# Gate granules shared by the two chunks of a pair, the second chunk one tile behind

## The chip, the cores and the metric

The kernel runs on one core of a Trainium2 chip. The metric is device time of one execution in microseconds (us). Before the change three executions took 1790.26, 1792.09 and 1793.38 us; their median is 1792.09 us.

## What is computed

Two residual layers over a sequence of 2048 rows of width 1024, in float32. Each layer is a token mixer (layer 0: a gated short convolution, layer 1: a gated causal pooling), followed by a gated embedding:

```python
for i in range(DEPTH):                       # DEPTH = 2
    hn = rmsnorm(h, norm_mix[i])
    h = h + (short_conv_mixer if i == 0 else pool_mixer)(hn, ...)
    gate = jax.nn.sigmoid(rmsnorm(h, ple_norm[i]) @ ple_w_gate[i])
    h = h + gate * (p[i] @ ple_w_proj[i])
return rmsnorm(h, final_norm)
```

The change concerns the product with `ple_w_gate[i]`, a 1024 x 1024 matrix, called the gate below.

## The kernel before

Everything is held transposed: features on the 128 partitions, rows of the sequence along the free dimension. The sequence is cut into 4 chunks of 512 columns; the two halves of the outer loop (`sc`) take two chunks each, so there are four pairs: layer 0 and layer 1 of each half. A float32 product is made of three float32r matmuls: both operands are split into a high and a low part (`mm`, L276 to L278, uses high x high, high x low, low x high).

Weights come in granules of 128 x 1024 (512 KB). A list, `order`, written out by hand, says in which order. `next_granule` takes the next one and loads ahead by `look[0]` granules: an SP DMA into one of 4 raw buffers, a cast on ACT for the high part (L117), a subtraction on DVE for the low part (L118). The split granules live in a ring of 4 buffers (`wring`), 8 KB per partition each.

Stages of one pair: the mixer's products, a filler (the products p @ w_proj of another chunk, evacuated by ACT, L763, and stored to DRAM), `mixer_out` (the mixer's output product for both chunks at once, adds into h on DVE, L727; it also makes the scaled split operands a[0], a[1] of the gate with L310 on ACT and L311 on DVE), the gates, another filler. `gate` runs one chunk: for each of 8 granules `dense_w` makes 24 matmuls of 128 x 128 by 128 x 512 into one PSUM bank, and `gate_out` evacuates it: multiply by the norm on DVE (L780), sigmoid on ACT (L781), times the embedding (fetched from DRAM, L782), add into h (L783). After that `Stat.add` accumulates squares (ACT L331, POOL L334), and a callback makes the operand for the next stage: in layer 0 a scaled split of h (L310, L311), in layer 1 of the first half `X.ahead`, which fetches one of 28 operands of the next half's mixer from DRAM (n<-ndr) and splits it (ACT L304, DVE L305). The second chunk's gate loads the same 8 granules again.

The root of a norm is made in two steps, `fin1` (ACT cast acc_hi L339, DVE L341, two matmuls `tot` L344, then L350 to L360 on DVE with L355 on POOL) and `fin2` (matmul `bc` L365, ACT copy `rb` L367). Both matmuls write the one bank of the PSUM pool `pst`. They are put into a list, `hooks`, and each `dense_w` runs the first one left in it. `mixer_out` leaves [fin2 of the first chunk, fin1 of the second, nop, fin2 of the second]. In layer 1 `finals` adds to fin2 eight scalings on DVE (L813), each with a store to the output.

The pools: 7 PSUM banks for products, 31 tiles of 4 KB per partition (`acts`) shared by h (4 tiles for a chunk), the split operands (one tile for each of 8 k's and chunk) and the next stage's operands; 4 buffers `nx` for tiles fetched from DRAM. The order within each engine's queue is drawn up by the tile framework at build time with a timeline simulation, from the order in which the program emits instructions; on the chip each engine but PE's weight load runs its queue in that order.

Of the kernel before, what the change touches and what calls it, by code (L numbers as in the profile page):

```python
# [18 lines left out]
T = 512  # L19
KT = D // P  # L20
NCH = S // T
# [28 lines left out]
def trunk_kernel(ctx: ExitStack, tc: tile.TileContext, xT, xN, pT, wts, par, out):  # L50
# [189 lines left out]
    for sc in range(2):  # L240
        order += filler_order(0, 2) if sc else []
        order += sum_order(sc, 4)
        for i in range(4, 2 * KT, 2):
            order += fold_order(i // 2 - FOLDS) if sc == 0 and FOLDS <= i // 2 < FOLDS + 4 else []
            order += [("sum", (sc, i + r, part)) for r in range(2) for part in range(4)]
        order += filler_order(0, 3) if sc else filler_order(1, 0)
        order += out_order(0)
        order += [("w", W_GATE[0] + i) for t in range(2) for i in range(KT)]
        order += filler_order(1, 1 + sc)
        order += [g for j in B_ORDER for g in (("comb", j), ("w", W_BZ + j))]  # L250
        order += out_order(1)
        order += [("w", W_GATE[1] + i) for t in range(2 - sc) for i in range(KT)]
    order += [("p", 2 * NCH - 1)]
    for h in range(2):
        order += [("pt", W_GATE[1] + 8 + h)] + [("w", W_GATE[1] + 4 * h + i) for i in range(4)]
# [52 lines left out]
    def split_scaled(h, gcol):  # L308
        a = new_act()
        nc.scalar.activation(out=a[:, 0, :], in_=h, func=AF.Copy, scale=pcol(gcol))  # L310
        nc.vector.scalar_tensor_tensor(out=a[:, 1, :], in0=h, scalar=pcol(gcol), in1=a[:, 0, :].bitcast(F32),  # L311
                                       op0=ALU.mult, op1=ALU.subtract)
        return a
# [237 lines left out]
    class Operands:  # L551
# [5 lines left out]
        def ahead(self, n):  # L557
            for name in self.have:
                while n and len(self.have[name]) < 4:
                    self.have[name].append(self.make(name, len(self.have[name])))  # L560
                    n -= 1
# [204 lines left out]
    def filler(layer, ch, *between):  # L766

        keys = filler_order(layer, ch)
        pt = next_granule(keys[0])
        for h in range(2):  # L770
            ple_half(layer, ch, pt, next_granule(keys[1 + h]), h)
            for f in between[h:h + 1]:
                f()
# [24 lines left out]
    def gate(layer, ch, a, hs, s_in, extra):  # L798
        s = Stat()
        held = []  # L800
        for k in range(KT):
            held.append((k, dense(("w", W_GATE[layer] + k), a), embedded(layer, ch, k)))
            if s_in.rb is None:
                continue
            for kk, g_ps, e in held:
                gate_out(g_ps, e, hs[kk], s_in.rb, 0, T)
                s.add(hs[kk])
                extra(kk)
            held = []
        return s  # L810

    def scale_out(ch, hs, rb, k, c0, c1):
        nc.vector.scalar_tensor_tensor(out=hs[k][:, c0:c1], in0=hs[k][:, c0:c1], scalar=pcol(G_FIN + k), in1=rb,  # L813
                                       op0=ALU.mult, op1=ALU.mult)
        nc.sync.dma_start(out=out[ch, :, k, c0:c1], in_=hs[k][:, c0:c1])

    def finals(ch, hs, s):
        def last():
            s.fin2()
            for k in range(KT):  # L820
                scale_out(ch, hs, s.rb, k, 0, T)
        return [s.fin1, nop, last]

    def gate_last(layer, ch, a, hs, s_in):
        pt = next_granule(("p", layer * NCH + ch))
        base = W_GATE[layer]
        half = T // 2
        ss = [Stat(half), Stat(half)]
        held, ws, wps, roots = [], {}, {}, []
        whole = KT // 2  # L830
        seq = [(k, None) for k in range(whole)]
        for i in range(whole, KT + LAG):
            if i < KT:
                seq.append((i, 0))
            if i >= whole + LAG:
                seq.append((i - LAG, 1))

        on_pool = (1, 3)

        def root(hf):  # L840
            c0, c1 = hf * half, (hf + 1) * half
            for k in on_pool:
                nc.scalar.activation(out=hs[k][:, c0:c1], in_=hs[k][:, c0:c1], func=AF.Copy, scale=pcol(G_FIN + k))
            bc = ss[hf].fin_fast(hs[KT - 1][:, c0:c1])
            rb = rbp.tile([P, T], F32, tag="rb", name="rb")
            nc.scalar.copy(out=rb[:, :half], in_=bc)
            return bc, rb

        def finish(hf, bc, rb, after=None):
            c0, c1 = hf * half, (hf + 1) * half  # L850
            for q in range(2):
                if after:
                    with tc.issue_after(after[q].ins):
                        scaled(hf, c0, c1, bc, rb, q)
                else:
                    scaled(hf, c0, c1, bc, rb, q)

        def scaled(hf, c0, c1, bc, rb, q):
            o = acts.tile([P, 4, half], F32, tag="act", name="o")
            for i in range(4):  # L860
                k = 4 * q + i
                if k in on_pool:
                    nc.gpsimd.tensor_tensor(out=o[:, i, :], in0=hs[k][:, c0:c1], in1=rb[:, :half], op=ALU.mult)
                else:
                    nc.vector.scalar_tensor_tensor(out=o[:, i, :], in0=hs[k][:, c0:c1], scalar=pcol(G_FIN + k),
                                                   in1=bc, op0=ALU.mult, op1=ALU.mult)
            if q == 0:
                nc.sync.dma_start(out=out[ch, :, 0:4, c0:c1], in_=o)
            else:
                for i in range(0, 4, 2):  # L870
                    nc.sync.dma_start(out=out[ch, :, 4 + i:6 + i, c0:c1], in_=o[:, i:i + 2, :])

        def span(hf):
            return (0, T) if hf is None else (hf * half, (hf + 1) * half)

        for k, hf in seq:
            if not hf:
                if k % 4 == 0:
                    wps[k // 4] = next_granule(("pt", base + 8 + k // 4))
                ws[k] = next_granule(("w", base + k))  # L880
            held.append((k, hf) + gate_mm(ws[k], wps[k // 4], pt, a, k, *span(hf)))
            if s_in.rb is None:
                continue
            for kk, h2, g_ps, p_ps in held:
                done = gate_out(g_ps, p_ps, hs[kk], s_in.rb, *span(h2))
                for q in (0, 1) if h2 is None else (h2,):
                    b0, b1 = span(q)
                    if kk == KT - 1:
                        roots.append(root(q))
                    else:  # L890
                        ss[q].add(hs[kk][:, b0:b1], nc.vector)
            held = []
        finish(0, roots[0][1][:, :half], roots[0][1], (done, ss[1].diagonal))
        finish(1, *roots[1])
# [61 lines left out]
    def keep(ch, hs, k):  # L956
        nc.sync.dma_start(out=h_dram[ch][:, k, :], in_=hs[k])

    for sc in range(2):
        chs = (2 * sc, 2 * sc + 1)  # L960
        Y = Outputs(2 * sc, (0, 1, 2, 3))
        mixer_a(sc, X, Y, xT[chs[1]])
        filler(*((0, 3) if sc else (1, 0)))
        a, hs, s = mixer_out(0, Y, xT[chs[0]])
        ab, ss = ([], []), []
        for t, ch in enumerate(chs):
            def after_gate(k):
                ab[t].append(split_scaled(hs[t][k], G_MIX + 8 + k))
                keep(ch, hs[t], k)

            ss.append(gate(0, ch, a[t], hs[t], s[t], after_gate))
            if t == 0:
                hooks.extend([ss[0].fin1, nop, ss[0].fin2])
        filler(1, 1 + sc, ss[1].fin1, ss[1].fin2)

        Y = Outputs(2 * sc + 1, (3, 2, 1, 0))
        mixer_b(ab, ss, Y, sc, nop if sc else between_b, h_dram[chs[1]])
        a, hs, s = mixer_out(1, Y, h_dram[chs[0]])
        if sc == 0:
            X = Operands(second_operand)  # L980

        def ahead(k):
            if sc == 0 and (t == 0 or k % 2):
                X.ahead(1)

        for t, ch in enumerate(chs):
            if ch == NCH - 1:
                look[0] = 1
                gate_last(1, ch, a[t], hs[t], s[t])
                break  # L990
            g = gate(1, ch, a[t], hs[t], s[t], ahead)
            if t == 0:
                hooks.extend(finals(ch, hs[t], g))
                continue
            fin1, _, fin2 = finals(ch, hs[t], g)
            filler(0, 2, fin1, fin2)


# [53 lines left out]
```

## Time and profile before

| | |
|---|---|
| median of 3 executions | 1792.09 us |
| the profiled execution | 1793.33 us |
| its span, first to last instruction | 1791.6 us |
| mean granted clock of PE | 0.995 |
| PE busy | 1757.7 us, 98% |
| DVE busy | 1360.8 us, 76% |
| ACT busy | 757.6 us, 42% |
| DMA traffic | 329.71 MB, mean 184 GB/s |

Busy times are added up over instructions of one engine; PE's matmuls overlap each other. PEld is the weight load of PE. "Idle" of an instruction is the time its engine stood still just before it, and the arrow names what ended that.

### The profile page before, as it was taken

The numbers are of one execution on the slowest core, as the hardware profiler recorded it, in microseconds if no ns is written. First come the engines' busy times: TensorE is split into PE (matmuls) and PEld (weight loads), VectorE is DVE, ScalarE is ACT, GpSimd is POOL, SyncE is SP. The second block draws the span as 40 slices with busy tenths as digits, with TensorE's granted clock in tenths as the row PEclk, the third lists the DMA queues.
The fourth block names the chain that finished last, engine by engine and source line by source line (L and its number), as shares of the span: only waits on it lengthen the run. The fifth ranks groups of instructions, "written<-read, shape, count | busy, mean of one in ns | idle before, by whom it ended". The sixth has DMA issues, their size and how long they took to land.

```text
span 1791.6 us, 21940 instructions
## 1 busy us (share of the span) xinstructions
PE 1757.7 (98%) x7883; PEld 1451.8 (81%) x7883; DVE 1360.8 (76%) x1876; ACT 757.6 (42%) x1142; POOL 230.0 (13%) x216
## 2 busy tenths in 40 slices
PE   9899999999999999999999999999999999999997
PEld 6688888888888888887878888888888888888787
DVE  6897787987987778889786555557798776578876
ACT  6734443355554311455553333334555511135542
POOL 1000000002322000023210000000132200002320
PEclk9999999999999999999999999999999999999998
DMA  9456566795465556844584434348536522365322
GB/s 347 170 185 220 205 233 222 279 361 170 141 200 177 187 190 224 296 146 139 198 270 142 137 104 141 102 160 296 199 125 199 189 95 97 109 223 171 129 90 95
DMA packets 123934, 329.71 MB, mean 184 GB/s; under 512 B 13744, under 2 KB 15792, under 8 KB 123824
## 3 DMA queue, kind: packets, MB, share of 16 engines
q1 hardware_dynamic: 123824, 328.30, 53.1%
q8 instruction: 62, 1.02, 0.2%
q14 instruction: 48, 0.39, 0.1%
HBM read 230.73 MB, written 97.52 MB: 183 GB/s over the span
## 4 chain that ended last, share of the span: by engine, by line
PE 77%; DVE 12%; DMA 5%; issue 3%; ACT 2%; POOL 0%; SPq 0%; DVEq 0%; ACTq 0%; POOLq 0%
PE mm L276 26%; PE mm L277 25%; PE mm L278 25%; DVE w L118 3%; DVE act L311 2%; DVE act L305 2%; DMA n<-ndr 1%; DVE h L727 1%; DMA sdo<-n 1%; ACT w L117 1%; DMA pdr<-wk 1%; DMA n<-in_wts_dram 1%; DMA raw<-in_wts_dram 0%; DVE dg L360 0%; DVE h L579 0%
## 5 line engine op out<-in xcount | busy, mean ns | idle before, releaser
L277 PE MATMUL mm<-act,w 128*128 128x512 f32 (+1 forms) x2400 | 930.7, 388 | 6.0 <-DVE act L305 3.6
L276 PE MATMUL mm<-act,w 128*128 128x512 f32 (+1 forms) x2400 | 923.8, 388 | 4.8 <-ACT wk L436 2.7
L278 PE MATMUL mm<-act,w 128*128 128x512 f32 (+1 forms) x2400 | 920.3, 387 | 0.0
L276 PEld LDWEIGHTS mm<-act,w 128*128 128x128 f32 x2400 | 452.0, 188 | 100.0 <-ACT wk L436 5.1
L277 PEld LDWEIGHTS mm<-act,w 128*128 128x128 f32 x2400 | 451.6, 188 | 100.3 <-DVE act L305 4.9
L278 PEld LDWEIGHTS mm<-act,w 128*128 128x128 f32 x2400 | 451.7, 188 | 91.8 <-issue 0.7
L117 ACT CAST w<-raw 128x1024 fp32r<-128x1024 f32 (+1 forms) x291 | 290.3, 1002 | 499.8 <-PE mm L278 341.0
L118 DVE TENSOR_TENSOR w<-raw,w 128x1024 fp32r<-128x1024 f32 (+1 forms) x291 | 347.2, 1197 | 102.3 <-ACT w L117 98.5
L334 POOL TENSOR_TENSOR acc<-acc,wk 128x512 f32<-128x512 f32 x97 | 139.0, 1433 | 473.4 <-ACT wk L331 473.4
L311 DVE SCALAR_TENSOR_TENSOR act<-h,par_sb,act 128x512 fp32r<-128x512 f32 x108 | 109.9, 1021 | 28.4 <-ACT act L310 26.2
L441 DVE TENSOR_TENSOR wk<-mm,wk 128x512 f32<-128x512 f32 x96 | 66.0, 689 | 85.0 <-PE mm L278 78.8
L331 ACT ACTIVATE wk<-h 128x512 f32<-128x512 f32 (+1 forms) x117 | 70.1, 602 | 102.2 <-DVE h L783 102.2
L310 ACT ACTIVATE act<-h,par_sb 128x512 fp32r<-128x512 f32 x108 | 77.0, 718 | 76.2 <-DVE h L727 72.8
L727 DVE TENSOR_TENSOR h<-mm,h 128x512 f32<-128x512 f32 x112 | 76.1, 685 | 26.1 <-PE mm L278 25.9
L305 DVE TENSOR_TENSOR act<-n,act 128x512 fp32r<-128x512 f32 x112 | 78.1, 724 | 19.2 <-ACT act L304 19.1
L304 ACT CAST act<-n 128x512 fp32r<-128x512 f32 x112 | 65.9, 620 | 61.5 <-DMA n<-ydr 37.5
L436 ACT COPY wk<-mm 128x512 f32<-128x512 f32 x96 | 54.9, 587 | 84.5 <-PE mm L278 81.6
L512 DVE SCALAR_TENSOR_TENSOR wk<-wk,par_sb 128x512 f32<-128x512 f32 x64 | 44.4, 748 | 34.3 <-ACT wk L510 34.3
L697 DVE TENSOR_TENSOR wk<-wk 128x526 f32<-128x526 f32 (+5 forms) x80 | 55.5, 694 | 2.3
L712 ACT ACTIVATE wk<-wk 128x512 f32<-128x512 f32 x32 | 20.2, 631 | 77.3 <-DVE wk L710 77.2
L781 ACT ACTIVATE wk<-wk 128x512 f32<-128x512 f32 (+1 forms) x68 | 40.8, 602 | 25.4 <-DVE wk L780 25.4
L710 DVE TENSOR_TENSOR wk<-mm,rb 128x512 f32<-128x512 f32 x32 | 22.0, 688 | 38.3 <-PE mm L278 38.3
(126 smaller groups left out, 1291.4 us busy)
## 6 DMA issues: line engine op xcount, KB each, us to landing
raw<-in_wts_dram SPq DMA_DIRECT2D x156, 512.0 KB, 3.8
n<-ydr SPq DMA_DIRECT2D x84, 256.0 KB, 4.3
ydr<-y SPq DMA_DIRECT2D x32, 512.0 KB, 3.5
raw<-in_wts_dram SPq DMA_DIRECT2D x64, 256.0 KB, 3.2
raw<-sdo SPq DMA_DIRECT2D x32, 512.0 KB, 6.0
raw<-sda SPq DMA_DIRECT2D x32, 512.0 KB, 3.8
pdr<-wk SPq DMA_DIRECT2D x56, 256.0 KB, 6.1
n<-pdr SPq DMA_DIRECT2D x56, 256.0 KB, 3.6
```

The source lines that it names most:

```text
L117: nc.scalar.copy(out=hi[:, c], in_=raw[:, c])
L118: eng.tensor_tensor(out=lo[:, c], in0=raw[:, c], in1=hi[:, c].bitcast(F32), op=ALU.subtract)
L276: nc.tensor.matmul(out=ps, lhsT=wh, rhs=ah, start=first, stop=False, skip_group_check=skip)
L277: nc.tensor.matmul(out=ps, lhsT=wh, rhs=al, start=False, stop=False, skip_group_check=skip)
L278: nc.tensor.matmul(out=ps, lhsT=wl, rhs=ah, start=False, stop=last, skip_group_check=skip)
L305: nc.vector.tensor_tensor(out=a[:, 1, :], in0=y, in1=a[:, 0, :].bitcast(F32), op=ALU.subtract)
L310: nc.scalar.activation(out=a[:, 0, :], in_=h, func=AF.Copy, scale=pcol(gcol))
L311: nc.vector.scalar_tensor_tensor(out=a[:, 1, :], in0=h, scalar=pcol(gcol), in1=a[:, 0, :].bitcast(F32), op0=ALU.mult, op1=ALU.subtract)
L331: nc.scalar.activation(out=sq, in_=h, func=AF.Square)
L334: (eng or nc.gpsimd).tensor_tensor(out=acc, in0=acc, in1=sq, op=ALU.add)
L441: nc.vector.tensor_tensor(out=o[:, 2:2 + T], in0=ps, in1=c, op=ALU.add)
L727: nc.vector.tensor_tensor(out=hs[t][k], in0=ps, in1=hs[t][k], op=ALU.add)
```

## The change

For three pairs (both layers of the first half, layer 0 of the second) one function, `gate_pair`, replaces the two calls of `gate`. Its products run in the order (granule 0, chunk 0), (1, 0), (0, 1), (2, 0), (1, 1), ... (7, 0), (6, 1), (7, 1). Each granule is loaded once. The look-ahead is 2 granules for the first six and 3 for the last two. The first chunk's norm is put into `hooks` after product (7, 0) without a nop between its steps, so that its fin1 follows (6, 1) and its fin2 (in layer 1 with the eight scalings) follows (7, 1). The fourth pair stays as it was.

```diff
-        order += [("w", W_GATE[0] + i) for t in range(2) for i in range(KT)]
+        order += [("w", W_GATE[0] + i) for i in range(KT)]
...
-        order += [("w", W_GATE[1] + i) for t in range(2 - sc) for i in range(KT)]
+        order += [("w", W_GATE[1] + i) for i in range(KT)]
...
+    def gate_pair(layer, sc, a, hs, s_in, extra, done):
+
+        ss, held, ws = [None, None], ([], []), {}
+        for k, t in [(0, 0)] + [(k - t, t) for k in range(1, KT) for t in range(2)] + [(KT - 1, 1)]:
+            if t == 0:
+                look[0] = 2 if k < KT - 2 else LOOK
+                ws[k] = next_granule(("w", W_GATE[layer] + k))
+            held[t].append((k, dense_w(ws[k], a[t]), embedded(layer, 2 * sc + t, k)))
+            if s_in[t].rb is None:
+                continue
+            for kk, g_ps, e in held[t]:
+                gate_out(g_ps, e, hs[t][kk], s_in[t].rb, 0, T)
+                if kk == 0:
+                    ss[t] = Stat()
+                ss[t].add(hs[t][kk])
+                extra(t, kk)
+            held[t].clear()
+            if (k, t) == (KT - 1, 0):
+                done(ss[0])
+        return ss
...
-        for t, ch in enumerate(chs):
-            def after_gate(k):
-                ab[t].append(split_scaled(hs[t][k], G_MIX + 8 + k))
-                keep(ch, hs[t], k)
-
-            ss.append(gate(0, ch, a[t], hs[t], s[t], after_gate))
-            if t == 0:
-                hooks.extend([ss[0].fin1, nop, ss[0].fin2])
+        ab = [], []
+
+        def after_gate(t, k):
+            ab[t].append(split_scaled(hs[t][k], G_MIX + 8 + k))
+            keep(chs[t], hs[t], k)
+
+        ss = gate_pair(0, sc, a, hs, s, after_gate, lambda g: hooks.extend([g.fin1, g.fin2]))
...
+        if sc == 0:
+            def ends(t, g):
+                fin1, _, fin2 = finals(chs[t], hs[t], g)
+                return fin1, fin2
+
+            def ahead(t, k):
+                if t == 0 or k % 2:
+                    X.ahead(1)
+
+            g = gate_pair(1, sc, a, hs, s, ahead, lambda g: hooks.extend(ends(0, g)))
+            filler(0, 2, *ends(1, g[1]))
+        else:
+            g = gate(1, chs[0], a[0], hs[0], s[0], nop)
+            hooks.extend(finals(chs[0], hs[0], g))
+            look[0] = 1
+            gate_last(1, chs[1], a[1], hs[1], s[1])
```

## Rows read from the trace of the kernel before

**Rows 1.** The page: engines' busy time (share) xinstructions, and chain shares by engine.

```profile
PE 1757.7 (98%) x7883; PEld 1451.8 (81%) x7883; DVE 1360.8 (76%) x1876; ACT 757.6 (42%) x1142; POOL 230.0 (13%) x216
PE 77%; DVE 12%; DMA 5%; issue 3%; ACT 2%; POOL 0%; SPq 0%; DVEq 0%; ACTq 0%; POOLq 0%
```

**Rows 2.** Windows: stretch, length, busy PE, PEld, DVE, ACT, POOL, clock, DMA share, GB/s.

```profile
462.00:558.00 96.00, 95.00 (x419) 78.28 (x418) 84.78 (x106) 51.42 (x77) 28.00 (x19) 1.00 0.52 169
816.00:909.00 93.00, 90.60 (x399) 74.28 (x398) 78.68 (x104) 46.73 (x70) 25.76 (x17) 1.00 0.57 187
909.00:936.00 27.00, 23.93 (x97) 18.96 (x96) 23.10 (x31) 20.35 (x36) 6.24 (x5) 0.94 0.84 267
1317.00:1413.00 96.00, 95.03 (x419) 78.33 (x418) 84.82 (x107) 51.95 (x77) 28.37 (x19) 1.00 0.52 172
```

**Rows 3.** Timeline of PE, starts of pairs 1, 2, 3: start, us, line, [idle before].

```profile
468.55 0.40 PE L365 MATMUL bc<-dg,ones_r 128*128 128x512 f32 x1
474.24 0.39 PE L276 MATMUL mm<-act,w 128*128 128x512 f32 x1
474.47 0.39 PE L277 MATMUL mm<-act,w 128*128 128x512 f32 x1
475.86 0.51 PE L344 MATMUL tot<-acc_hi,ones_r 128*128 128x512 f32 x1 [1.00 <-ACT rb L367]
...
830.20 0.50 PE L344 MATMUL tot<-acc_hi,ones_r 128*128 128x512 f32 x1 [1.00 <-ACT rb L367]
846.87 0.47 PE L365 MATMUL bc<-dg,ones_r 128*128 128x512 f32 x1 [1.40 <-DVE dg L360]
...
1331.98 0.50 PE L344 MATMUL tot<-acc_hi,ones_r 128*128 128x512 f32 x1 [0.97 <-ACT rb L367]
```

**Rows 4.** Timeline of ACT at the start of pair 1.

```profile
473.75 0.62 ACT L339 CAST acc_hi<-acc 128x512 fp32r<-128x512 f32 x1 [2.03 <-DVE acc L334]
474.28 1.04 ACT L117 CAST w<-raw 128x1024 fp32r<-128x1024 f32 x1
475.23 0.58 ACT L367 COPY rb<-bc 128x512 f32<-128x512 f32 x1
```

**Rows 5.** Timeline of DVE, starts of pairs 1 and 2.

```profile
472.38 0.74 DVE L311 SCALAR_TENSOR_TENSOR act<-h,par_sb,act 128x512 fp32r<-128x512 f32 x1
474.41 0.69 DVE L341 TENSOR_TENSOR acc_lo<-acc,acc_hi 128x512 fp32r<-128x512 f32 x1 [0.69 <-ACT acc_hi L339]
...
833.68 0.69 DVE L305 TENSOR_TENSOR act<-n,act 128x512 fp32r<-128x512 f32 x1 [2.08 <-ACT act L304]
837.35 1.23 DVE L118 TENSOR_TENSOR w<-raw,w 128x1024 fp32r<-128x1024 f32 x1 [0.44 <-ACT w L117]
841.61 1.21 DVE L118 TENSOR_TENSOR w<-raw,w 128x1024 fp32r<-128x1024 f32 x1
846.04 0.68 DVE L360 TENSOR_TENSOR dg<-fold,rs 128x512 fp32r<-128x512 f32 x1
```

**Rows 6.** Timeline of PE after pair 2's gates.

```profile
920.02 0.50 PE L276 MATMUL mm<-w 128*128 128x512 f32 x1 [1.16 <-ACT wk L763]
932.27 0.56 PE L276 MATMUL mm<-act,w 128*128 128x512 f32 x1 [1.91 <-ACT wk L763]
933.06 0.63 PE L278 MATMUL mm<-act,w 128*128 128x512 f32 x1
933.49 0.63 PE L276 MATMUL mm<-act,w 128*128 128x512 f32 x1
```

**Rows 7.** Timeline of ACT and DVE around the end of pair 2.

```profile
928.77 1.93 ACT L304 CAST act<-n 128x512 fp32r<-128x512 f32 x3 [3.37 <-DMA n<-ndr]
931.65 2.03 ACT L763 COPY wk<-mm 128x512 f32<-128x512 f32 x4
893.42 6.43 DVE L813 SCALAR_TENSOR_TENSOR h<-h,par_sb,rb 128x512 f32<-128x512 f32 x8
939.58 0.69 DVE L360 TENSOR_TENSOR dg<-fold,rs 128x512 fp32r<-128x512 f32 x1
```

**Rows 8.** Windows of line L305 alone, the splits of the next half's operands.

```profile
816.00:909.00 93.00, 7.53 (x12) 1.00 0.57 187
909.00:945.00 36.00, 12.94 (x16) 0.95 0.78 255
```

More of the change, by code (lines that the diff above doesn't have):

```diff
@@ L964, in trunk_kernel @@
         a, hs, s = mixer_out(0, Y, xT[chs[0]])
-        ab, ss = ([], []), []
-        for t, ch in enumerate(chs):
-            def after_gate(k):
-                ab[t].append(split_scaled(hs[t][k], G_MIX + 8 + k))
-                keep(ch, hs[t], k)
-            ss.append(gate(0, ch, a[t], hs[t], s[t], after_gate))
-            if t == 0:
-                hooks.extend([ss[0].fin1, nop, ss[0].fin2])
+        ab = [], []
[3 more added lines that the diff above has]
+        ss = gate_pair(0, sc, a, hs, s, after_gate, lambda g: hooks.extend([g.fin1, g.fin2]))
         filler(1, 1 + sc, ss[1].fin1, ss[1].fin2)
@@ L980, in trunk_kernel @@
             X = Operands(second_operand)
[L982 to L996, printed above, removed]
+        if sc == 0:
[12 more added lines that the diff above has]
+            gate_last(1, chs[1], a[1], hs[1], s[1])
 def kernel(x, p, norm_mix, a_w_in, a_w_conv, a_w_out, b_w_in, b_w_grp, b_scale, b_w_out,
```

## The prediction

> **What bounds the kernel now.** I read the page's busy shares first. PE is busy 98% of the span, DVE 76%, ACT 42%; the chain that ended last runs 77% through PE [rows 1]. So the change can win or lose only where PE stands still, and the next view is a table of windows over the three stretches that it touches. In the two layer 0 pairs PE is busy 95.00 and 95.03 of 96 us; in pair 2 (layer 1, first half) 90.60 of 93, and in the 27 us behind its gates 23.93, at a granted clock of 0.94 [rows 2]. DMA is at 0.52 to 0.57 in the gates. The whole of PE's idle time there is 1.0 + 2.4 + 1.0 + 3.1 = 7.5 us, and that is the size of the game: 0.4% of 1792 us.
>
> The timeline of PE tells where it lies. Matmuls start 0.227 us apart (474.24 and 474.47), so one product of 24 takes 5.44 us. Each pair has a wait of 1.00, 1.00 and 0.97 us before `tot`, the first matmul of the second chunk's root, released by the copy rb on ACT; pair 2 has another of 1.40 us before `bc`, released by DVE's L360 [rows 3]. The idle column counts from a modelled end 0.39 us after the last start; the next matmul could have started 0.23 us after it, so each wait loses 0.16 us more: 1.16, 1.16, 1.13 and 1.56 us, together 5.0. Behind pair 2's gates PE waits 1.16 and 1.91 us for L763, the filler's evacuation on ACT [rows 6], which is 1.32 + 2.07 us in the same count. After the second wait matmuls start 0.43 us apart (933.06, 933.49: the 1.2 GHz level); my count there is 9 of them, 9 x (0.43 - 0.23) = 1.8 us. So 5.2 us are lost at that place.
>
> **What the change removes.** 24 granules of 512 KB with their casts (L117, 1.04 us of ACT [rows 4]) and subtractions (L118, 1.2 us of DVE [rows 5]): 8 in each pair, 8.3 us of ACT and 9.7 us of DVE out of stretches in which ACT is busy about half and DVE 79 to 85% [rows 2]. PE's 48 products in the three pairs are the same, so no term comes of this by itself: beside PE that work is hidden. It counts only where it stands ahead of something PE waits for.
>
> *Start of each pair.* ACT runs acc_hi 473.75, then a granule's cast at 474.28, then rb at 475.23 [rows 4]; `tot` needs acc_hi and, since the pool `pst` has one bank, the end of rb. The cast between them is the fifth granule's: the ring of 4 buffers lets it in when product (0, 0) has read the first. In the new order the first granule is read until (0, 1) ends, 5.4 us later, so this cast can't stand there. Then rb starts 0.95 us earlier (475.23 - 474.28), and `tot` at about 474.9. I take 0.95 us for each of three pairs, 2.85 us. Ends: 0 (another instruction takes its place ahead of rb) and 1.16.
>
> *The wait of pair 2 before bc.* `tot` runs at 830.20, L360 at 846.04; in between DVE does two such subtractions, 1.23 + 1.21 us, and stands 2.08 us for a fetched operand [rows 5]. The subtractions go (later granules come one in 10.9 us instead of 5.44). That is more than the 1.56 us lost, but the build-time order will also put bc earlier in PE's queue, and the 2.08 us stay. I take half, 0.8 us; ends 0 and 1.56.
>
> **What it adds.** *The second chunk's operands are needed earlier*: product (0, 1) comes third, not ninth. The last tile of a[1] is finished by L311 at 472.38 + 0.74 = 473.1 [rows 5]; (0, 1) starts at about 475 and uses that tile in its last three matmuls, 21 x 0.227 = 4.8 us later. Slack 6.5 us; I cost it at nothing. Were the cover gone, everything beyond 6.5 us would be PE idle time.
>
> *Look-ahead of 2.* A granule's buffer is freed four products before the granule that gets it is used, 21.8 us; cast and subtraction take 2.3. Nothing. For the last two granules the look-ahead is 3 with five granules alive; the fourth buffer is free after (5, 1), still 16 us ahead of use.
>
> *The pool of 31 tiles.* h takes 8, a[0] and a[1] 16, and now none of the 16 is free before (7, 0), the 14th product, ends. Before, a[0] went after the eighth. In layer 0 h's tiles are freed behind the stores, so only the 14th new tile is held up, by one product. In pair 2 h stays: 7 of the 12 operands of the next mixer fit, the other 5 must wait for (7, 0), 10.9 us before the gates end. PE doesn't need them until the filler is over, 21.8 us after (7, 0). Nothing on PE's path directly.
>
> *End of each pair.* The roots of both chunks now follow each other: fin1 and fin2 of the first behind (6, 1) and (7, 1), fin1 of the second after half the filler. So the second's `tot` comes close behind the first's `bc` in the single bank, the neighbourhood that costs 1.16 us at the starts today. Where the roots are 40 us apart, as at the ends of today's first chunks, I found no such wait. Between 0 and 1.16 us at each of three ends I take 0.3, nearer to none, because the filler gives PE other work to put between: 0.9 us.
>
> *The finals of pair 2.* The first chunk's eight scalings, 6.43 us of DVE at 893.42 [rows 7], move from the middle of the second chunk's gates into the filler, with their 8 stores of 256 KB in SP's queue, and 5 late splits at 12.94/16 = 0.81 us [rows 8] move near them. Queued behind the stores on SP are the fetches of the next mixer's operands; behind the scalings on DVE their splits L305. On the other side the gates' own tail is no longer late when the filler begins. The wait of 1.91 us came from ACT: L763 stood behind three L304, which waited 3.37 us for a fetch [rows 7]. These fetches stay. So I take the 5.2 us lost there as unchanged; ends: all 5.2 us won, or the pile-up of the rival below.
>
> The Trainium skill's page "TensorE: Matmul & The Clock Gate", section "HAM oscillation — how this bites in real kernels", says that idle stretches drop PE to half its clock, which it keeps until it has been busy again. The trace agrees: 0.94 over [rows 2] and the 0.43 us spacing behind the 1.91 us wait [rows 6], at 1.00 behind the waits of about 1 us. By that rule a longer wait at the end of pair 2 would be paid about twice.
>
> **Sum.** -2.85 - 0.8 + 0.9 + 0 = -2.75 us. The profiled execution took 1793.33 us (span 1791.6), 1.24 above the median of the three, so 1790.6 there and 1789.3 us for the median.
>
> **Rivals.** *A, the end of pair 2 clears as well.* For it: with DVE and ACT less loaded in the gates the tail ends sooner, and L763 would not stand behind it; the scalings no longer push the last gates. Against: L304 still waits for fetches. Price: -3.65 + 0.9 - 5.2 = -8.0 us, 1784.1 us. Chance 0.20.
>
> *B, a pile-up behind pair 2 (slower).* In the 27 us after the gates DVE has 27 - 23.10 = 3.9 us free [rows 2]; the change puts 6.43 us of scalings and 5 x 0.81 = 4.0 us of splits there, 10.5 in all, so 6.6 us do not fit. It decides where the next mixer's 13th operand, needed after 10.9 us of filler and 13.6 us of products, isn't split in time, or an evacuation stands behind such a split. Then PE waits up to 6.6 us, with 1.8 us again at the lower clock: 8.4 in place of nothing, -2.75 + 8.4 = +5.6, 1797.7 us. Against: the second scalings may come later (today's second root ends at 939.58 [rows 7], 30 us after the gates), and 24.5 us of other PE work cover the 10.5. Chance 0.17.
>
> *C, the waits only move.* The bank's wait of 1.16 us leaves the three starts and turns up at the three ends, where both roots now meet: -3.65 + 3 x 1.16 = -0.2 us, 1791.9 us. For it: the same three instructions (acc_hi, another one, rb) share ACT there. Against: the filler. Chance 0.18.
>
> **How the numbers follow.** The forecast has 0.45, with its own range of 1786 to 1792 us. About 0.2%, 3.6 us, is what can be told from no change. Faster by more: all of A and two fifths of the forecast, 0.20 + 0.18 = 0.38. Slower by more: nearly all of B and a little of C and of what I have not seen, 0.19. The rest, 0.43, lies within. The range goes from A's value to a little short of B's: 1783.5 to 1796.5 us.
>
> **What would show it.** Loads of 512 KB granules fall by 24, L117 and L118 by 24 instructions each, PE's 7883 stay. At the starts `tot` has under 0.3 us of idle time before it and no L117 stands between acc_hi and rb; the wait before pair 2's `bc` is under 1.4 us. The first `mm` of (0, 1) has no idle time before it: if it has, the slack of 6.5 us was wrong. At the ends, idle time before a `tot` released by rb speaks for C; idle time before the next mixer's products released by L305, L436 or L763, with a longer stretch at the lower clock, for B; no idle time from the filler on, for A. PE idle time inside the gates, before a product's first matmul, would mean that the 31 tiles or the 7 banks bind, which the sum takes as nothing.

## Result and profile after

The changed kernel takes 1812.74 us (median of four executions, 1810.55 to 1815.12) against 1792.74 us for the kernel before in the same comparison (1790.26 to 1795.84). The ratio is 1.0113, with a 95% interval of 1.01 to 1.0125: slower by 20 us, where 3 us less were forecast. The time lies outside the predicted range and above rival B's.

Two lines of the page after: the engines (answering to the first line of [rows 1]), and one of the costliest groups, whose last column is the idle time before it and what ended most of it.

```profile
PE 1766.9 (98%) x7883; PEld 1456.0 (80%) x7883; DVE 1334.0 (74%) x1852; ACT 738.3 (41%) x1118; POOL 231.2 (13%) x216
...
L276 PE MATMUL mm<-w 128*128 128x512 f32 (+1 forms) x144 | 50.7, 363 | 14.1 <-ACT wk L763 9.3
```

What was to be removed is removed. PE's instructions are the same 7883; DVE and ACT have 24 each fewer, which are L118 and L117 (291 to 267); SP's loads of 512 KB granules fall from 156 to 132. DVE is busy 26.8 us less, ACT 19.3 us less. The last line is the new thing: the filler's matmuls (`mm<-w`, 144 in all) are preceded by 14.1 us of idle time, 9.3 of it ended by the filler's evacuation L763 on ACT. Before it was 1.2 us.

To see where 20 us arise, follow one landmark through both traces: the `bc` at the start of each of the four pairs. Its weight load stands at 468.3, 822.7, 1324.5 and 1677.0 us before, at 467.9, 828.5, 1337.7 and 1695.2 after; the spans are 1791.6 and 1811.7. The lag is -0.4, +5.8, +13.2, +18.2 and +20.1 us. So pair 1 loses 6.2 us, pair 2 7.4, pair 3 5.0, and pair 4, whose code is the old one, 1.9.

Windows of the kernel after, 9 us each at the places of the loss (columns as in [rows 2]; the two from 558.00 are pair 1's end, the three from 918.00 pair 2's, then pair 3's end and pair 4's start):

```profile
558.00:567.00 9.00, 5.67 (x22) 4.18 (x21) 6.79 (x9) 6.26 (x11) 3.99 (x4) 0.87 0.41 138
567.00:576.00 9.00, 9.00 (x31) 7.14 (x31) 3.05 (x3) 4.60 (x8) 0.00 (x0) 0.76 0.65 218
918.00:927.00 9.00, 5.19 (x22) 3.65 (x20) 7.21 (x11) 5.11 (x8) 3.21 (x2) 0.97 0.56 173
927.00:936.00 9.00, 5.06 (x11) 3.31 (x12) 8.90 (x14) 5.51 (x11) 1.97 (x2) 0.50 0.78 244
936.00:945.00 9.00, 9.00 (x33) 7.24 (x32) 8.35 (x12) 4.78 (x7) 4.20 (x1) 0.78 0.99 342
1431.00:1440.00 9.00, 5.66 (x19) 4.03 (x18) 5.12 (x7) 5.78 (x10) 2.00 (x3) 0.81 0.57 202
1719.00:1728.00 9.00, 7.53 (x26) 6.05 (x27) 6.86 (x10) 4.68 (x7) 2.59 (x2) 0.81 0.55 175
```

The same stretches of the kernel before that have no row above (pair 1's end, pair 2's end, and pair 4's start, which then lay 18 us earlier):

```profile
558.00:567.00 9.00, 9.00 (x42) 7.44 (x41) 4.88 (x6) 7.42 (x12) 1.84 (x2) 1.00 0.70 258
567.00:576.00 9.00, 9.00 (x41) 7.43 (x40) 7.27 (x15) 1.50 (x4) 1.84 (x2) 1.00 0.74 236
918.00:927.00 9.00, 7.84 (x35) 6.16 (x34) 8.38 (x10) 7.06 (x12) 1.89 (x2) 1.00 0.86 285
927.00:936.00 9.00, 7.09 (x24) 5.34 (x23) 6.14 (x11) 6.87 (x14) 1.65 (x1) 0.81 0.94 307
936.00:945.00 9.00, 9.00 (x41) 7.41 (x40) 4.52 (x8) 3.69 (x5) 0.00 (x0) 1.00 0.61 222
1701.00:1710.00 9.00, 7.57 (x33) 6.31 (x34) 6.88 (x9) 4.69 (x7) 2.61 (x2) 1.00 0.52 175
```

Read the first bracket, the matmuls started in the window, at 0.227 us each. Pair 1's end starts 22 + 31 = 53 where it started 83: 30 short, 6.8 us. Pair 2's end starts 66 where it started 100: 34 short, 7.7 us. Pair 3's end starts 19; full windows here have 41 or 42, so 22 short, 5.0 us. Pair 4's start has 26 in place of 33: 1.6 us. Together 21.1 us, against a lag of 20.1 in which the starts' gain of about 1.6 is already taken off. So nearly the whole loss lies at the ends of the three changed pairs, with a small echo in pair 4, and the clock column shows where a part of it comes from: 0.50 to 0.97 where it was 1.00 or 0.81.

Now the chain of one end, pair 1's. PE after, columns as in [rows 3]. The last product's matmuls end at 551.75, where the filler's begin:

```profile
552.43 0.40 PE L344 MATMUL tot<-acc_hi,ones_r 128*128 128x512 f32 x1
553.81 0.40 PE L344 MATMUL tot<-acc_lo,ones_r 128*128 128x512 f32 x1
...
562.09 0.48 PE L365 MATMUL bc<-dg,ones_r 128*128 128x512 f32 x1 [0.16 <-DVE dg L360]
565.74 0.79 PE L276 MATMUL mm<-w 128*128 128x512 f32 x1 [3.17 <-ACT wk L763]
566.33 0.63 PE L277 MATMUL mm<-w 128*128 128x512 f32 x1
566.76 0.63 PE L278 MATMUL mm<-w 128*128 128x512 f32 x1
```

PE fills all seven banks with products of the filler and then waits 3.17 us for the first L763; behind the wait matmuls run at the 1.2 GHz level, 0.63 us each by the profile, and start 0.43 us apart (566.33, 566.76). DVE there:

```profile
553.03 1.23 DVE L118 TENSOR_TENSOR w<-raw,w 128x1024 fp32r<-128x1024 f32 x1 [1.99 <-ACT w L117]
554.25 0.69 DVE L350 TENSOR_TENSOR wk<-tot,fold 128x512 f32<-128x512 f32 x1
554.86 0.68 DVE L780 TENSOR_TENSOR wk<-mm,rb 128x512 f32<-128x512 f32 x1
...
557.58 0.68 DVE L780 TENSOR_TENSOR wk<-mm,rb 128x512 f32<-128x512 f32 x1
...
560.16 1.79 DVE L360 TENSOR_TENSOR dg<-fold,rs 128x512 fp32r<-128x512 f32 x1
```

The two L780 are the evacuations of the last two products, (6, 1) and (7, 1). Product (6, 1) was finished at about 546.3, a product's 5.44 us before the gates' end, so its evacuation comes 8.5 us after it, though DVE stood idle for 1.99 us in that time. It stands right behind L350, the first step of the root that needs `tot`. The row puts the idle time down to a granule's cast, whose L118 stands ahead of L350; but L350 could not have begun sooner in any case, since the second `tot` matmul ends at 553.81 + 0.40 = 554.21. ACT ends the chain:

```profile
562.61 0.59 ACT L367 COPY rb<-bc 128x512 f32<-128x512 f32 x1 [1.96 <-PE bc L365]
563.97 0.63 ACT L331 ACTIVATE wk<-h 128x512 f32<-128x512 f32 x1 [0.78 <-DVE h L783]
564.51 0.71 ACT L310 ACTIVATE act<-h,par_sb 128x512 fp32r<-128x512 f32 x1
565.12 2.03 ACT L763 COPY wk<-mm 128x512 f32<-128x512 f32 x4
```

The filler's four copies stand behind rb and behind the squares (L331) and operand (L310) of product (7, 1), both late because that product's evacuation was. Pair 3 shows the same, and pair 2 the same order with one more thing in it. PE's waits there:

```profile
922.28 0.50 PE L276 MATMUL mm<-w 128*128 128x512 f32 x1 [0.75 <-DVE wk L780]
928.00 0.79 PE L276 MATMUL mm<-w 128*128 128x512 f32 x1 [4.06 <-DVE wk L780]
934.51 0.80 PE L276 MATMUL mm<-w 128*128 128x512 f32 x1 [2.94 <-ACT wk L763]
...
1435.53 0.79 PE L276 MATMUL mm<-w 128*128 128x512 f32 x1 [3.17 <-ACT wk L763]
```

In pair 2 the second `tot` matmul ends at 917.0, but L350 starts only at 920.95: splits of fetched operands stand ahead of it, and DVE waits 1.81 us for their casts, which had themselves waited 2.41 us for a fetch. So the last 4 us of that delay are not those of `tot`:

```profile
919.67 1.36 DVE L305 TENSOR_TENSOR act<-n,act 128x512 fp32r<-128x512 f32 x2 [1.81 <-ACT act L304]
920.95 0.68 DVE L350 TENSOR_TENSOR wk<-tot,fold 128x512 f32<-128x512 f32 x1
921.55 0.68 DVE L780 TENSOR_TENSOR wk<-mm,rb 128x512 f32<-128x512 f32 x1
```

### The profile page after: what moved, and what is told of

The parts are those of the page before. It is cut to its first block, busy times and chain, and to the rows that moved or that the text cites. A ratio compares the mean times of both kernels' runs of the same rounds, so it can differ in the third digit from the quotient of the medians.

```text
span 1811.7 us, 21829 instructions
## 1 busy us (share of the span) xinstructions
PE 1766.9 (98%) x7883; PEld 1456.0 (80%) x7883; DVE 1334.0 (74%) x1852; ACT 738.3 (41%) x1118; POOL 231.2 (13%) x216
## 4 chain that ended last, share of the span: by engine, by line
PE 64%; DVE 9%; issue 2%; DMA 2%; ACT 2%; POOL 1%; DVEq 0%; ACTq 0%; POOLq 0%
PE mm L276 21%; PE mm L278 21%; PE mm L277 21%; DVE w L118 2%; DVE act L311 2%; DVE act L305 2%; DVE h L727 1%; DMA n<-ndr 1%; ACT w L117 1%; POOL r L355 0%; DVE dg L360 0%; DVE rs L357 0%; DMA n<-pdr 0%; PE tot L344 0%; ACT wk L331 0%
## 5 line engine op out<-in xcount | busy, mean ns | idle before, releaser
L117 ACT CAST w<-raw 128x1024 fp32r<-128x1024 f32 (+1 forms) x267 | 265.3, 998 | 501.9 <-PE mm L278 364.3
L118 DVE TENSOR_TENSOR w<-raw,w 128x1024 fp32r<-128x1024 f32 (+1 forms) x267 | 315.8, 1187 | 94.7 <-ACT w L117 93.7
L331 ACT ACTIVATE wk<-h 128x512 f32<-128x512 f32 (+1 forms) x117 | 70.1, 602 | 93.3 <-DVE h L783 93.3
L310 ACT ACTIVATE act<-h,par_sb 128x512 fp32r<-128x512 f32 x108 | 77.0, 718 | 74.9 <-DVE h L727 72.8
L305 DVE TENSOR_TENSOR act<-n,act 128x512 fp32r<-128x512 f32 x112 | 76.2, 707 | 25.4 <-ACT act L304 25.3
L436 ACT COPY wk<-mm 128x512 f32<-128x512 f32 x96 | 54.9, 588 | 85.8 <-PE mm L278 82.1
L781 ACT ACTIVATE wk<-wk 128x512 f32<-128x512 f32 (+1 forms) x68 | 41.1, 604 | 63.6 <-DVE wk L780 63.4
L276 PE MATMUL mm<-w 128*128 128x512 f32 (+1 forms) x144 | 50.7, 363 | 14.1 <-ACT wk L763 9.3
L780 DVE TENSOR_TENSOR wk<-mm,rb 128x512 f32<-128x512 f32 (+1 forms) x68 | 44.2, 652 | 16.4 <-PE mm L278 16.3
```

Of the source, the lines that this page charges most:

```text
L117: nc.scalar.copy(out=hi[:, c], in_=raw[:, c])
L118: eng.tensor_tensor(out=lo[:, c], in0=raw[:, c], in1=hi[:, c].bitcast(F32), op=ALU.subtract)
L276: nc.tensor.matmul(out=ps, lhsT=wh, rhs=ah, start=first, stop=False, skip_group_check=skip)
L305: nc.vector.tensor_tensor(out=a[:, 1, :], in0=y, in1=a[:, 0, :].bitcast(F32), op=ALU.subtract)
L331: nc.scalar.activation(out=sq, in_=h, func=AF.Square)
```

## Experiments

Why does L780 of a finished product stand behind the root's L350? The order in which the program queues DVE's instructions, around pair 1's end of the kernel after (queue number, line, tiles with their numbers):

```
612 L341 acc_lo_4702 <- acc_4100, acc_hi_4700
613 L118 w_4778 <- raw_4776, w_4778
614 L350 wk_4707 <- tot_4704, fold8_101
615 L780 wk_4721 <- mm_4675, rb_4228      product (6, 1)
620 L780 wk_4764 <- mm_4733, rb_4228      product (7, 1)
```

L350's result `own` and L780's result are tiles of the same pool, `wk`, with ten buffers (the tile numbers grow in the order in which the program emits them; 613, of another pool, stands ahead although it was emitted later). `own` is emitted inside product (6, 1), by the hook, ahead of that product's `gate_out`, of (7, 1)'s, and of the filler's eight copies. Theory T: the pool gives its buffers out in the order of emission, so whoever comes after `own` in the pool is queued behind it; what holds L350 (its `tot`, which needs the squares of (7, 0)) holds the last evacuations and through them the filler. Rival F: the root's second step, `bc` and rb on ACT, is what blocks ACT's copies. Rival S: sharing the granules, the interleaved order of the products itself, costs it. Beside the experiments the kernel before was measured again, at 1792.61 us (e1, e2, e4, e5) and 1792.66 us (e3, e6, e7, e8); the ratios are to it.

**e1_roots_in_filler.** Both roots emitted after all gate products:

```diff
-        ss = gate_pair(0, sc, a, hs, s, after_gate, lambda g: hooks.extend([g.fin1, g.fin2]))
-        filler(1, 1 + sc, ss[1].fin1, ss[1].fin2)
+        ss = gate_pair(0, sc, a, hs, s, after_gate, nop)
+        filler(1, 1 + sc, ss[0].fin1, both(ss[0].fin2, ss[1].fin1, ss[1].fin2))
...
-            g = gate_pair(1, sc, a, hs, s, ahead, lambda g: hooks.extend(ends(0, g)))
-            filler(0, 2, *ends(1, g[1]))
+            g = gate_pair(1, sc, a, hs, s, ahead, nop)
+            fs = ends(0, g[0]) + ends(1, g[1])
+            filler(0, 2, fs[0], both(*fs[1:]))
```

> The first chunk's root leaves the hooks: its fin1 comes after half of the filler, its fin2 and the second chunk's fin1 and fin2 after the other half; all else as in the changed kernel. Theory T (the root's scratch tile 'own', L350, is taken from the pool wk ahead of the tiles of the last two gate evacuations and of the filler's eight copies, and the pool gives its tiles out in that order, so all of these wait for the root's first matmul): the waits of 3.2 us and the low clock behind the gates go in all three pairs, 5 to 7 us each, time 1790 to 1796. Rival S (the loss is in the interleaving itself: two tails, eight scalings and late operands pile up on DVE): 1805 or more. Rival F (fin2's copy rb stands ahead of the filler's copies on ACT): as T, 1790 to 1796, so this run tells S from the other two.

Measured: 1787.4 us, ratio 0.9973 (0.996 to 0.9987). DVE at pair 1's end:

```profile
548.86 0.68 DVE L780 TENSOR_TENSOR wk<-mm,rb 128x512 f32<-128x512 f32 x1
...
552.52 0.68 DVE L780 TENSOR_TENSOR wk<-mm,rb 128x512 f32<-128x512 f32 x1
...
560.37 0.68 DVE L350 TENSOR_TENSOR wk<-tot,fold 128x512 f32<-128x512 f32 x1
```

Both evacuations now run ahead of the root, and no wait of PE for L763 or L780 is left anywhere. The whole loss is gone, and 5 us more, with the products still interleaved: S falls. T and F both stand.

**e2_second_step_late.** Only fin2 of the first chunk moves out of the hooks; fin1 stays where the change put it:

```diff
-        ss = gate_pair(0, sc, a, hs, s, after_gate, lambda g: hooks.extend([g.fin1, g.fin2]))
-        filler(1, 1 + sc, ss[1].fin1, ss[1].fin2)
+        ss = gate_pair(0, sc, a, hs, s, after_gate, lambda g: hooks.append(g.fin1))
+        filler(1, 1 + sc, both(ss[0].fin2, ss[1].fin1), ss[1].fin2)
```

(and the same in layer 1).

> Only fin2 of the first chunk moves, from behind product (7, 1) to half of the filler; fin1 stays behind (6, 1). Theory T: the scratch tile still stands ahead of the last evacuations, so nothing is won, 1808 to 1815. Rival F: rb is no longer ahead of the filler's copies, 1790 to 1797. Rival S: 1805 to 1815 as well.

Measured: 1811.76 us, ratio 1.0105 (1.0089 to 1.0121): nothing comes back, F falls. DVE at pair 1's end has the order of the kernel after, about 1 us later:

```profile
555.31 0.69 DVE L350 TENSOR_TENSOR wk<-tot,fold 128x512 f32<-128x512 f32 x1
555.91 0.68 DVE L780 TENSOR_TENSOR wk<-mm,rb 128x512 f32<-128x512 f32 x1
```

**e4_own_pool.** The changed kernel with everything where it was, but `own` from a pool of its own; the number of buffers stays ten in all:

```diff
-    wk = ctx.enter_context(tc.tile_pool(name="wk", bufs=10))
+    wk = ctx.enter_context(tc.tile_pool(name="wk", bufs=9))
+    ownp = ctx.enter_context(tc.tile_pool(name="ownp", bufs=1))
...
-            own = wtile()[:, :T].rearrange("p (a b) -> p a b", b=64)
+            own = ownp.tile([P, T], F32, tag="own", name="own").rearrange("p (a b) -> p a b", b=64)
```

> The changed kernel with the root's scratch tile in a pool of its own (one buffer), wk cut from 10 to 9 buffers; hooks as in the changed kernel. Theory T: L780 of the last two products no longer follows L350, the waits behind the gates go, 1789 to 1796, though both roots still meet at the end of the pair. Rivals F and S: the hooks and the interleaving are untouched, 1805 to 1815.

Measured: 1794.32 us, ratio 1.001 (1.0 to 1.002). This alone gives back 1812.7 - 1794.3 = 18.4 of the 20 us. DVE at the same place (one line added, so L781 is L780 of the others and L351 is L350), and the windows of PE answering to those of the kernel after:

```profile
550.15 0.68 DVE L781 TENSOR_TENSOR wk<-mm,rb 128x512 f32<-128x512 f32 x1
...
553.82 0.68 DVE L781 TENSOR_TENSOR wk<-mm,rb 128x512 f32<-128x512 f32 x1
...
558.22 0.68 DVE L351 TENSOR_TENSOR own<-tot,fold 128x512 f32<-128x512 f32 x1
```

```profile
558.00:567.00 9.00, 9.00 (x41) 7.48 (x40) 6.16 (x11) 7.47 (x14) 3.50 (x3) 1.00 0.69 240
1431.00:1440.00 9.00, 9.00 (x41) 7.44 (x40) 4.52 (x9) 2.27 (x3) 2.49 (x3) 1.00 0.19 58
918.00:927.00 9.00, 6.54 (x29) 5.10 (x28) 8.36 (x14) 8.02 (x16) 4.27 (x3) 1.00 0.81 255
```

The ends of pairs 1 and 3 are full again, at full clock. T is shown: only the pool of one tile was changed, and the queue's order, the waits and the time went with it. One wait of 2.46 us for the filler's copies is left in pair 2. There the copies stand on ACT behind splits (L305 here), two of which had waited 2.30 and 1.93 us for fetches. This is the kind of wait that [rows 7] shows, and not the pool's:

```profile
918.98 0.62 ACT L305 CAST act<-n 128x512 fp32r<-128x512 f32 x1 [1.93 <-DMA n<-ndr]
...
921.50 2.51 ACT L764 COPY wk<-mm 128x512 f32<-128x512 f32 x5
```

**e5_before_own_pool.** The same pool in the kernel before, as a control for the pool and its ninth buffer.

> The kernel before with the same own pool for the root's scratch tile (wk 9 buffers). Theory T: there the pool's order held up one evacuation per root, covered by 7 banks, so little changes: within 3 us of the kernel before. It is the base against which e4 says what the change itself is worth: T expects e4 equal to this run or up to 4 us faster (the starts); S expects e4 10 us or more slower.

Measured: 1795.36 us, ratio 1.0014 (1.0005 to 1.0022). The kernel before has L350 ahead of L780 too, but gains nothing from parting them; it even loses a little, the waits for L360 before `bc` being 5.5 us in all against 3.4. The interleaved kernel of e4 is 1 us faster than this one, which can't be told from no difference: with the pool's order out of the way in both, the change itself is worth 1 us or nothing.

**e3_before_late_root.** The kernel before, the first chunk's root delayed until just before its second chunk's gates end, where the change has it:

```diff
-                hooks.extend([ss[0].fin1, nop, ss[0].fin2])
+                hooks.extend([nop] * 6 + [ss[0].fin1, ss[0].fin2])
```

(and the same in layer 1 of the first half).

> The kernel before (two separate gates, granules loaded twice), only the first chunk's root moved: its fin1 behind the seventh product of the second chunk, its fin2 behind the eighth, as late as in the changed kernel; three pairs. Theory T (the root's scratch tile is handed out ahead of the last evacuations' and the filler's tiles): the loss comes back without any sharing or interleaving; the last product's evacuation waits for L350 as there, 3 to 7 us a pair, 1800 to 1813. Rival S (interleaving or sharing is needed for the loss): within 4 us of the kernel before.

Measured: 1797.41 us, ratio 1.0017 (1.0006 to 1.0027). T's number was wrong, and rival S's, for a loss that needs the interleaving, is nearer. In this kernel's trace pairs 1 and 3 lose nothing, and pair 2 about 2 us, behind the gates, where the eight scalings now lie and ACT's copies stand behind a split that waited for the store of a scaled tile (another 1.1 us lie ahead of pair 1 and 1.6 us in pair 4, where nothing was moved):

```profile
923.92 5.38 DVE L813 SCALAR_TENSOR_TENSOR h<-h,par_sb,rb 128x512 f32<-128x512 f32 x8
```

```profile
933.21 0.62 ACT L304 CAST act<-n 128x512 fp32r<-128x512 f32 x1 [2.28 <-DMA out_dram<-h]
933.73 2.04 ACT L763 COPY wk<-mm 128x512 f32<-128x512 f32 x4
```

So `own`'s place alone isn't enough. In the old order the first chunk's squares are complete some 29 us before this root: in pair 1 POOL ends the last at 519.2, and `tot` starts at 548.0, 5.9 us ahead of the filler (in the kernel after 0.7 us behind its start). L350 runs as soon as DVE reaches it and holds nobody. The loss needs both: the pool's order (e4), and the interleaving (this run), which by the traces acts through a root whose inputs are only just being made. What e3 does show is a small version of rival B, about 2 us.

**e6_granules_twice.** e1 with the interleaved products, but each granule loaded again for the second chunk:

```diff
-        for k, t in [(0, 0)] + [(k - t, t) for k in range(1, KT) for t in range(2)] + [(KT - 1, 1)]:
-            if t == 0:
-                look[0] = 2 if k < KT - 2 else LOOK
-                ws[k] = next_granule(("w", W_GATE[layer] + k))
-            held[t].append((k, dense_w(ws[k], a[t]), embedded(layer, 2 * sc + t, k)))
+        for k, t in PAIR:
+            held[t].append((k, dense(("w", W_GATE[layer] + k), a[t]), embedded(layer, 2 * sc + t, k)))
```

(`PAIR` is the same list of products; the three entries of `order` follow it.)

> As e1 (interleaved gates, roots in the filler), but every granule is loaded, cast and split for each chunk again, with the look-ahead of 3. What is left of the difference to e1 is what sharing the granules is worth by itself. Hidden work (the prediction's view, beside PE): the cast is back ahead of rb at the starts, so 0.5 us at each of three starts and DVE's wait before bc, 1 to 3 us slower than e1, 1788 to 1791. If sharing is what pays: back to the kernel before, 1792 or more.

Measured: 1788.74 us, ratio 0.9972 (0.9961 to 0.9983), the same as e1. SP's granule loads are 156 again. So the 24 saved loads, casts and subtractions are worth nothing that can be measured; what e1 gains comes from the order of the products, of the roots or both, which no run parts.

**e7_start_later and e8_before_start_later.** To take the waits before `tot` away, a nop between the first chunk's fin2 and the second's fin1, in e1 and in the kernel before:

```diff
-        hooks.extend([s[0].fin2, s[1].fin1, nop, s[1].fin2])
+        hooks.extend([s[0].fin2, nop, s[1].fin1, nop, s[1].fin2])
```

> As e1, with one nop more in the hooks that the mixer leaves, so that the second chunk's fin1 and fin2 come one product later at the start of each pair. If PE's waits at the starts (0.5 us before tot in three pairs, 1.0 in the fourth, 1.25 and 1.8 us before bc) come from the root standing in PE's queue before its inputs are ready, most of them go: 1 to 4 us faster than e1, 1783 to 1786. If the queue order drawn up at build time moves with it and leaves the same waits: as e1, 1787.

> The kernel before with the same nop. It tells whether what e7 wins depends on the shared granules: if not, 1 to 4 us faster than the kernel before, 1788 to 1791; if the cast ahead of rb still decides there, within 1 us of it.

Measured: e7 1787.74 us, ratio 0.9968 (0.9955 to 0.998), not told apart from e1; e8 1799.07 us, ratio 1.0032 (1.0021 to 1.0043), slower, which neither of its two expectations had. PE's waits in e8's trace, and the longest of them, at pair 2:

```profile
PE bc L365 <- DVE dg L360: 10.0, 4, 4.5
```

```profile
852.15 0.58 PE L365 MATMUL bc<-dg,ones_r 128*128 128x512 f32 x1 [4.52 <-DVE dg L360]
```

The waits before `tot` are gone, 3.9 us in all, as meant; but the waits before `bc` rise from 3.4 to 10.0 us. `tot` stands about 4 us later and `bc` waits for what follows it on DVE: 1.38, 4.52 and 1.38 us at pairs 1 to 3, where it was 0, 1.40 and 0 [rows 3]. A stall on a chain moves along it when only one link is shifted. In e7 the same nop costs less (1.05 us at pair 2, none at 1 and 3). That DVE has fewer subtractions there would explain it, but no run shows that alone.

e1 and e7 are the best: 5 us (0.27% and 0.32%) under the kernel before. Between the second chunks' `tot` at the four starts and the span's end (475.86, 830.20, 1331.98, 1684.45, 1791.6 before; 474.14, 828.19, 1325.54, 1678.80, 1785.6 in e1) the gain is 1.7 us ahead of pair 1, 0.3 in pair 1, 4.4 in pair 2, -0.8 in pair 3 and 0.4 in the rest. Pair 2's is the end that rival A spoke of: of [rows 6]'s two waits for L763 none is left there, only one of 0.65 us for L436, and the clock of that stretch stays at 1.00.

## Why the prediction was wrong

**The step that failed** is the one about the end of each pair. I weighed only the neighbourhood of the two roots in their one bank and took 3 x 0.3 = 0.9 us. The three ends lost 6.8 + 7.7 + 5.0 = 19.5 us more than before, pair 2's 7.7 on top of the 5.2 lost there already; with the root's scratch tile out of the shared pool (e4) 18.4 us of the 20 came back. I counted the root as two matmuls and some DVE instructions; I did not ask which pool its scratch tile comes from, who is emitted behind it in that pool, and when its inputs are ready. The last point could be read off the order of the products: (7, 0), whose squares the root needs, now has two products behind it, where the first chunk's last product used to have eight. The pool's order is visible in the trace of before, where L350 stands ahead of L780 too; there it does no harm:

```profile
522.25 0.69 DVE L350 TENSOR_TENSOR wk<-tot,fold 128x512 f32<-128x512 f32 x1
522.86 1.28 DVE L780 TENSOR_TENSOR wk<-mm,rb 128x512 f32<-128x512 f32 x2
```

Two evacuations run back to back behind the root: one had waited for it. The sum took the seven banks as binding nothing; I named PE idle time in the gates as the sign against that, and it came in the filler instead, as waits for L780 and L763.

**The clock** added to it. Behind waits of 3 to 4 us the granted clock of a window is 0.50 to 0.87 and matmuls start 0.43 us apart, the 1.2 GHz level. In pair 1 the wait costs 3.17 + 0.16 us (as counted for [rows 3]) and `bc`'s 0.16 + 0.16, together 3.65 of the 6.8; the rest, 3.1 us, is the lower clock (13 starts, about 0.2 us too far apart each, and the first one 0.36). In pair 3 the same waits leave 1.4 of the 5.0 us to it. The rule stands in the Trainium skill's page "TensorE: Matmul & The Clock Gate", section "HAM oscillation — how this bites in real kernels": idle stretches send PE to half its clock. The trace agrees, with the numbers above; "paid about twice", as the prediction has it, holds for pair 1 and not for pair 3. Pair 4's echo is of this kind: `bc` waits about as before (1.81 us after, 2.04 before), but this time the clock falls to 0.81 where it had stayed at 1.00.

**The starts.** The right cause, half the size: this term was mis-sized. No L117 stands between acc_hi and rb any more, and the waits before `tot` are 0.49, 0.48 and 0.49 us where [rows 3] has 1.00, 1.00 and 0.97: 0.5 us each in place of 0.95. In e1, which has the same start, acc_hi and rb follow each other directly:

```profile
472.99 0.62 ACT L339 CAST acc_hi<-acc 128x512 fp32r<-128x512 f32 x1 [2.03 <-DVE acc L334]
473.51 0.58 ACT L367 COPY rb<-bc 128x512 f32<-128x512 f32 x1
```

So rb does start 0.52 us behind acc_hi in place of 1.48, sooner by about the 0.95 us that I counted. But `tot` moved as well: counted from the first chunk's `bc` it is the 26th matmul of PE, where it was the 28th, and two matmuls of 0.227 us give back 0.45 of the 0.95 us. I had taken its place in PE's queue as fixed. In e6, where the granules are loaded twice, `tot` is the 28th again and the wait back at 0.99 us, so the removed cast did make the difference.

**Pair 2's wait before `bc`**: -0.8 us expected, 1.40 to 1.28 measured. L360 does come sooner behind `tot`, 12.5 us in place of 15.8, but `bc` moved up in PE's order by the same 3.3 us; I had named that and halved the gain for it; it took nearly all.

**The second chunk's operands, the look-ahead and the 31 tiles**: right (the slack, by its own numbers, is 6.7 us and not 6.5). PE has no wait at the first products of (0, 1), and none inside the gates of the three pairs other than those named and 0.17 us before pair 2's second `tot` matmul.

**The rivals.** A came true in e1 (4.4 us of the 5.2) and e6 (6.1 us), once the roots were out of the way, not in the change itself. B had the right sign, at the wrong place and of the wrong cause: pair 2's finals are not the reason, since pairs 1 and 3 lose nearly as much without any, and e1 has the same scalings behind the gates without loss; e3 shows B's mechanism at 2 us. C did not happen: no `tot` at the ends waits for rb.

Not settled: how the 7.7 us of pair 2 divide between the pool's order and the fetches ahead of L350; and the part of the 0.14% of e5 that belongs to the missing tenth buffer rather than to the changed order.

## What to carry to other kernels

When an instruction is moved, look at the pools its tiles come from as well as at its engine: a scratch tile taken early from a shared pool puts its later users behind it in the queue, and if its inputs are late, evacuations of finished products wait for it with PE's banks full. Give such a tile a pool of its own, or emit the work behind the evacuations, and check at each moved step when its inputs are complete in the new order. Removing hidden work (24 loads, 19 us of ACT, 27 us of DVE here) moved the time by nothing that could be measured; the order of what remained moved it by 25 us.

## What the runs showed of the hardware

Waits of PE of 1.0 to 1.4 us left its clock at 1.00 in the windows read. Of those between, 1.91 us before [rows 6] and 1.81 us after brought it down, 2.04 us at the start of pair 4 before and 2.46 us in e4 did not. Those of 3.17 us (twice) and 4.06 us after brought it down; the one of 2.94 us came while it was still down. What decides between the middle ones these runs don't settle.

L360, a DVE product of two operands of 128 x 512 elements, takes 0.69 us [rows 7], but 1.79 us at pair 1's end after, where a POOL addition ran beside it:

```profile
559.66 1.74 POOL L334 TENSOR_TENSOR acc<-acc,wk 128x512 f32<-128x512 f32 x1 [1.22 <-ACT wk L331]
```

It was issued at 560.16 and ended at 561.95, 0.55 us after that addition: as if nearly all of it had run behind the addition. Between 440 and 920 us of the traces before and after, five L360 were issued during such an addition, and all took 1.77 to 1.79 us and ended 0.55 us behind it; the other eight took 0.68 or 0.69 us. The Trainium skill's page "SBUF — State Buffer", section "Terms", says so: the pair of ports that DVE and GpSimd share is locked for a whole instruction and the other blocks. The trace agrees. Its 1.1 us lie on the way to `bc` here.
